# Second third's token tiles ahead of its weights, and the last two LRU blocks beside the attention's later heads

## The chip, the cores and the metric

The kernel runs on one core of a Trainium2 chip. The time is device microseconds of one execution. The engines are TensorE (PE; its weight loads are PEld), VectorE (DVE), ScalarE (ACT), GpSimd (POOL) and SyncE (SP, which issues nearly all DMAs).

## The reference, cut to what matters

One layer of a hybrid trunk, 2048 tokens of width 1024 with 16 meta tokens ahead of them, in float32. An input projection feeds three groups of heads; their outputs go together into an output projection, and a feed-forward layer follows.

```python
h += rms_norm(w_out @ concat(rg_lru_group, forgetting_attention_group, rwkv7_group), g_post)   # all read w_in @ rms_norm(h)
h += rms_norm(w_down @ (gelu(g) * v))            # [g | v] = causal_dwconv3(w_up @ rms_norm(h))

def rg_lru_group(xa, ya, ...):                   # the gated linear recurrence, 256 wide
    u = causal_dwconv(xa, conv_w) + conv_b       # 4 taps
    r = sigmoid(u @ ga_w + ga_b); i = sigmoid(u @ gx_w + gx_b)
    log_a = -8.0 * r * softplus(-lam)
    a = exp(log_a); b = sqrt(-expm1(2 * log_a)) * (i * u)
    h = scan(h_t = a_t * h_{t-1} + b_t)
    return h * gelu(ya)

def forgetting_attention_group(...):             # 8 heads of 64
    s = qh @ kh.T + (c_q - c_k)                  # c: running sum of log_sigmoid(f)
    return softmax(causal(s)) @ vh

def rwkv7_group(...):                            # 4 heads of 64, a state of 64 x 64 a head
    S = S * w_t - (S @ kk_t) (kk_t * a_t)^T + v_t k_t^T;  o_t = S @ r_t
```

## The kernel before

The work goes through five stages: input projection, attention, output projection, and the two halves of the feed-forward layer.

The input projection runs in three thirds of the tokens ("parts" 0 to 2; tiles of 128 tokens 0 to 7, 7 to 13, 13 to 17). For each third, `w_in_norm` loads token tiles (`token_load`), normalises them and transposes them on TensorE (L161). Then `w_in_part` takes the weight columns one after the other. In part 0 it splits each weight tile into a high and a low part and keeps both in memory (`scr_wk`); parts 1 and 2 load them back (L259, tiles `wh` and `wl`). The loads, and most stores, are issued by SP in the order in which they stand.

Beside the projection's matmuls run the recurrences. The tokens are cut in nine blocks, 0 to 8; the last is a short one of one chunk, 64 tokens. `recurrences` makes three blocks a third: the RWKV block (`R.block`, whose tail `R.ending` is run one block later) and the LRU block (`lru_block`). What is left over when the projection is written is written ahead of the attention, and `rec`, the group of memory pools that the recurrences use, is closed there.

An LRU block runs twice, for channels 0 to 127 and 128 to 255 (`p` 0 and 1). Each of the two passes loads its input (`rwlraw`, L1549), applies the convolution on ScalarE (L1556) and with three VectorE operations (L1558), two gate matmuls on TensorE (L1563, L1564), then some twenty operations on ScalarE and VectorE, among them a square root with a table of its own on ScalarE (L1579, the exponential's is loaded again after it), a scan on VectorE (L1581), the product with the second input (L1585 to L1590) and a store (L1591). The gates' result lies in a PSUM bank of the recurrences, `eps`.

The tail of an RWKV block, as far as it is spoken of here: solves with small matmuls (L1316), L1360 to L1412, the outputs (L1443, L1448), a normalisation on VectorE with an inverse square root of small steps (L76 to L84, L1453 to L1461), a transpose and a gate (L1468, L1472), L1475, L1479, L1480 and the store of the result (L1482).

The attention has two halves. Half 0 takes blocks 0 and 1 of 512 queries for all eight heads, half 1 blocks 2 and 3. For each head and block, `maxima` computes the row maxima of the scores (matmul L644 into a bank `mx`, VectorE L649, transpose L659, ScalarE L660), and `weights` computes the scores again (L773, L774, bank `sc`), their exponentials (ScalarE L778, tile `p`) and the product with the values (L796, bank `po`). From head 5 of half 0 on (`WIDE`), there are three `mx` banks instead of two. At each piece `Attn.tick` is called; every second tick takes a step of a generator `beside`, which in half 1 is the meta tokens' part.

The order on each engine is made ahead of the run by a scheduler: it takes the instructions in the order in which the code writes them, knows which waits for which and when memory comes free, and lets later work go ahead of work that waits. `issue_after(x)` keeps an instruction behind instruction `x`. Pools marked `early` may lie on memory whose former user is still at work; the first write then waits.

Of the kernel before, what the change touches and what calls it, by code (L numbers as in the profile page):

```python
# [1 line left out]

# [6 lines left out]
F32 = mybir.dt.float32  # L9
# [9 lines left out]
P = 128  # L19
# [13 lines left out]
class Core:  # L33


    def __init__(self, tc, ctx):
        self.tc = tc
        self.nc = tc.nc
        self.ctx = ctx
        self.uid = 0  # L40
        nc = self.nc
        self.const = ctx.enter_context(tc.tile_pool(name="const", bufs=1))
        self.ident = self.const.tile([P, P], F32, name="ident")
        make_identity(nc, self.ident[:])
        self.flip = 0
        self.root = self.apart = False
        self.power, self.held = None, []
        self.turns = 0
# [84 lines left out]
def token_load(core, pools, src, rows):  # L133

    xt = pools["nt"].tile([P, D], F32, tag="nt_x", name=core.n("xt"))
    core.nc.sync.dma_start(xt[:rows], src)
    return xt


# [96 lines left out]
def w_in_kept(scr, c0):  # L236

    return scr["wk"][c0 // P]


def w_in_weights(core, pools, w_in, c0, scr, part, raw=None, behind=False):

    src = w_in[:, c0 : c0 + P].rearrange("(k p) c -> p k c", p=P)
    if raw is not None:
        pair = hi, lo = [pools["w"].tile([P, KD, P], F32R, tag=s, name=core.n(s)) for s in ("wh", "wl")]
        core.loaded = core.nc.sync.dma_start(raw, src)
        with core.tc.issue_after(core.high.ins) if behind else nullcontext():
            core.rounded = core.nc.scalar.activation(hi[:], raw, AF.Copy)
        with core.tc.issue_after(core.low.ins) if behind else nullcontext():
            core.nc.vector.tensor_tensor(lo[:], raw, hi[:], op=ALU.subtract)  # L250
    elif part == 0:
        pair = split_load(core, pools["w"], (pools["nt"], "nt_x", None), src, [P, KD, P], "w")
    else:
        core.turns += part == 2
        pl, tags = (pools["nt"], ("nt_x", "nt_x")) if core.turns % 4 > 1 else (pools["w"], ("wh", "wl"))
        pair = [pl.tile([P, KD, P], F32R, tag=tag, name=core.n(s)) for s, tag in zip(("wh", "wl"), tags)]
    for t, kept in zip(pair, w_in_kept(scr, c0)):
        t = t[:].rearrange("p k c -> p (k c)").bitcast(F32)
        core.loaded = core.nc.sync.dma_start(*((kept, t) if part == 0 else (t, kept)))  # L259
    return pair  # L260


# [248 lines left out]
class Attn:  # L511
# [63 lines left out]
    def t(self, shape, tag, dt=F32, bufs=2):  # L575
        return self.pool.tile(shape, dt, tag=tag, name=self.core.n(tag), bufs=bufs)
# [335 lines left out]
    def run(self, pool, third):  # L912


        self.queue = self.nc.sync
        ready = []
        for half, bs in enumerate(((0, 1), (2, 3))):
            if half:
                self.rear(third, "k2_2")
                self.beside = self.meta(pool)  # L920
            for h in range(NH):
                self.wide = (half, h) >= WIDE
                with self.core.tc.issue_after(self.core.settled) if not half and h < 2 else nullcontext():
                    keys = self.keys(h, 4 * bs[-1] + 5)
                for b in bs:
                    gen, total, out = self.maxima(h, b, keys), self.pieces(b), []

                    def fill(share, gen=gen, total=total, out=out):
                        while len(out) < min(total, share * total):
                            out.append(next(gen))  # L930

                    if len(ready) == self.AHEAD:
                        self.weights(*ready.pop(0), fill)
                    fill(1.0)
                    ready.append((h, b, keys, next(gen)))
                    self.serial += 1
                    self.later.append((self.clock + self.FINISH, self.serial, lambda gen=gen: next(gen, None)))
                    self.later.sort(key=lambda x: x[:2])
                    if len(ready) < self.AHEAD + 1 and not half and h == 0:
                        next(gen)  # L940
        self.tail = True
        for i, step in enumerate(ready):
            if i == len(ready) - 1:
                self.queue = self.nc.gpsimd
            self.weights(*step, lambda share: None)
        self.flush()
        for _ in self.beside:
            pass
        while len(self.later) > 1:
            self.later.pop(0)[2]()  # L950
# [644 lines left out]

class Banks:


# [554 lines left out]
PACE = 1.25  # L2155

WIDE = (0, 5)

LATE, NORMS = 8, 2

# [35 lines left out]
def recurrences(core, R, lk, f_bias, scr, blocks, part):  # L2196


    for blk in blocks:
        gate_block(core, R, f_bias, scr, blk[2])  # L2200
        yield
    for b in ((0, 1, 2), (3, 4, 5), (6, 7, 8))[part]:
        gen = R.block(b)
        while next(gen) != R.SOLVED:
            yield
        yield from R.ending
        R.ending = gen
        yield from lru_block(core, R, scr, lk, b)


_INS = [
# [9 lines left out]
def hybrid_block_kernel(ctx: ExitStack, tc: tile.TileContext, args, out):  # L2221
    a = {s: v[0] if s != "meta_tokens" else v for s, v in args.items()}
    nc = tc.nc
    core = Core(tc, ctx)
    scr = scratch(tc, ctx, core)
# [8 lines left out]
    def pool(es, name, bufs, **kw):  # L2234
        return es.enter_context(tc.tile_pool(name=name, bufs=bufs, **kw))

    right = {"side": "right"}
    early = {"reuse_waits": "tile"}
# [8 lines left out]
    with ExitStack() as p1:  # L2247
# [2 lines left out]
        rec = ExitStack()  # L2250
        ps_rw = pool(rec, "ps_rw", 2, space=PSUM, **right)
        ps_ae = pool(rec, "ps_ae", 1, space=PSUM, **right)
        rc = pool(rec, "rc", 1, **right)
        gp = pool(rec, "gp", 1, **right)
        rp = pool(rec, "rp", 1, **right)
        with ExitStack() as p1a:
# [14 lines left out]
            for part in range(3):  # L2271
# [7 lines left out]
                if part == 0:  # L2279
# [5 lines left out]
                    with tc.issue_after(core.powered.ins):  # L2285
# [9 lines left out]
                            for s, v in a.items() if s.startswith("rwkv_")  # L2295
                        },
                    )
                    lk = lru_consts(
                        core, gp, ps_ae,
                        {  # L2300
# [8 lines left out]
                    R = Rwkv(core, rp, dp, ps_rw, ps_ae, scr, rk)  # L2309
# [30 lines left out]
        with ExitStack() as p1b:  # L2340
            more = pool(p1b, "ps_more", 1, space=PSUM, **right, **early)
            front = pool(p1b, "front", 2, **early)
            ps_at = pool(p1b, "ps_at", 1, space=PSUM, **early)
            ap = pool(p1b, "ap", 2, **early)
            with tc.issue_after(core.parted):
                at = Attn(core, ap, ps_at, more, scr, front)
            at.second = pool(p1b, "ap2", 1, **early)

            pool(p1b, "pad", 1, **right).tile([P, 23872], F32, name="pad")
            at.run(pool(p1b, "mt", 1, **right, **early), pool(p1b, "k2", 1, **right, **early))  # L2350
    qp = pool(ctx, "qp", 1, **early)
    gf = pool(ctx, "gf", 1, **early)
    with ExitStack() as p3:
# [12 lines left out]
        with p2:  # L2366
# [9 lines left out]
            for i, (f, rows) in enumerate(FFN_TILES):  # L2376
# [12 lines left out]
                for _ in range(NORMS if i > LATE else 0):  # L2389
                    if todo:  # L2390
                        q, f, rows = todo.pop(0)
                        xt = ffn_fetch(core, np_, scr, f, rows)
# [144 lines left out]
```

## Time and profile before

| What | Value |
|---|---|
| Runs, us | 2953.79, 2942.76, 2957.45 (median 2953.79) |
| Profiled execution, us | 2948.27, span 2946.6, mean granted clock 0.98 |
| Busy share of the span | PE 96%, PEld 83%, DVE 68%, ACT 51%, POOL 44% |
| Share of the chain that ended last | PE 69%, DVE 8%, DMA 5%, ACT 5% |
| First to second third of the projection | 258 to 292 us |
| Attention, half 0 | from 849 us, half 1 written from about 1068 us |

The times count from the span's start. A row of the timeline has start, length, engine, line, operation, and in brackets how long the engine was idle before it and what ended that. PEclk is the share of full speed that TensorE's clock was granted.

### The profile page before, as it was taken

The page shows a single profiled execution, that of the slowest core. Times are in us where ns is not written, and L with a number is a line of the kernel's source. Part 1 is how long each engine was busy: PE and PEld are TensorE (multiplying, and loading weights), DVE is VectorE, ACT ScalarE, POOL GpSimd, SP SyncE. Part 2 cuts the span into 40 slices and gives each one's busy share as a digit, 9 for nine tenths or more (in the row PEclk, how much of TensorE's full clock was granted, in tenths as well). Part 3 has the DMA queues.
Part 4 walks back from the last instruction along what each step waited for, and adds up shares of the span by engine and source line. Part 5 has one row for each costly group of instructions (what it writes and reads, how often), then busy time and mean ns, then how long its engine had stood idle before and what let it go on. Part 6 is the DMA issues. An engine that isn't in the chain of part 4 may idle for free.

```text
span 2946.6 us, 53222 instructions
## 1 busy us (share of the span) xinstructions
PE 2832.0 (96%) x18854; PEld 2441.3 (83%) x18854; DVE 1997.5 (68%) x3839; ACT 1504.0 (51%) x2937; POOL 1302.6 (44%) x1572
## 2 busy tenths in 40 slices
PE   8999999989988889999999999999999999999998
PEld 8998989978965555666578999999999999787887
DVE  4357654665678665556656988888787787656766
ACT  3246442554446554555645666666666665324333
POOL 1002221222114567667624666456655444656443
PEclk9999999999989899999999999999999999999999
DMA  7775678577643357445264665577767764436453
GB/s 244 250 243 190 220 232 289 181 234 244 204 122 79 79 130 222 100 121 128 49 192 148 210 195 179 157 231 210 220 200 223 215 198 148 141 112 218 151 171 122
DMA packets 470344, 530.51 MB, mean 180 GB/s; under 512 B 86863, under 2 KB 356889, under 8 KB 468525
## 3 DMA queue, kind: packets, MB, share of 16 engines
q1 hardware_dynamic: 469308, 526.18, 59.1%
q8 instruction: 148, 2.42, 0.4%
q0 software_dynamic: 768, 0.93, 0.1%
q14 instruction: 120, 0.98, 0.1%
HBM read 368.07 MB, written 158.90 MB: 179 GB/s over the span
## 4 chain that ended last, share of the span: by engine, by line
PE 69%; DVE 8%; DMA 5%; ACT 5%; issue 2%; POOL 2%; SPq 1%; DVEq 0%; POOLq 0%; ACTq 0%
PE psu L193 10%; PE psu L194 9%; PE psu L195 9%; PE psd L193 4%; PE psd L194 4%; PE psd L195 4%; PE po L796 4%; PE psp L193 2%; PE psp L195 2%; PE psp L194 2%; PE mx L644 2%; PE sc L773 2%; PE pswo L193 2%; PE pswo L194 2%; PE pswo L195 2%
## 5 line engine op out<-in xcount | busy, mean ns | idle before, releaser
L194 PE MATMUL psu<-xo,uw 128*128 128x344 f32 x1848 | 592.0, 321 | 0.0
L193 PE MATMUL psu<-xo,uw 128*128 128x344 f32 x1848 | 586.6, 322 | 3.3 <-DVE vb L1971 2.2
L195 PE MATMUL psu<-xo,uw 128*128 128x344 f32 x1848 | 582.4, 320 | 0.6 <-DVE uw L1780 0.6
L193 PE MATMUL psp<-xh,wh 128*128 128x384 f32 (+2 forms) x1152 | 379.9, 330 | 0.7 <-DMA wh<-scr_wk 0.7
L194 PE MATMUL psp<-xl,wh 128*128 128x384 f32 (+2 forms) x1152 | 374.8, 325 | 0.0
L195 PE MATMUL psp<-xh,wl 128*128 128x384 f32 (+2 forms) x1152 | 373.2, 324 | 0.0
L1780 DVE TENSOR_TENSOR uw<-uq,uw 128x512 fp32r<-128x512 f32 x341 | 313.6, 924 | 61.6 <-ACT uw L1779 58.1
L193 PEld LDWEIGHTS psu<-xo,uw 128*128 128x128 f32 x1848 | 346.1, 188 | 4.7 <-DVE vb L1971 2.7
L194 PEld LDWEIGHTS psu<-xo,uw 128*128 128x128 f32 x1848 | 347.4, 188 | 0.0
L195 PEld LDWEIGHTS psu<-xo,uw 128*128 128x128 f32 x1848 | 346.0, 188 | 1.4 <-DVE uw L1780 1.4
L1779 ACT ACTIVATE uw<-uq 128x512 fp32r<-128x512 f32 x462 | 287.8, 627 | 104.8 <-PE psu L195 46.0
L778 ACT ACTIVATE p<-sc,bias 128x512 f32<-128x512 f32 (+4 forms) x352 | 197.3, 590 | 161.6 <-PE sc L774 138.0
L649 DVE TENSOR_REDUCE mc<-mx 128x1 f32<-128x512 f32 (+5 forms) x352 | 191.6, 566 | 113.8 <-PE mx L644 81.0
L1919 DVE SCALAR_TENSOR_TENSOR uy<-psu,ffn_cols,uy 128x342 f32<-128x342 f32 (+1 forms) x390 | 220.8, 567 | 64.6 <-ACT uy L1917 62.2
L1927 POOL TENSOR_TENSOR uy<-uy,uy 128x342 f32<-128x342 f32 (+1 forms) x132 | 146.9, 1113 | 229.5 <-DVE uy L1919 69.3
L1780 POOL TENSOR_TENSOR uw<-uq,uw 128x512 fp32r<-128x512 f32 x121 | 184.8, 1527 | 132.6 <-ACT uw L1779 113.2
L193 PEld LDWEIGHTS psp<-xh,wh 128*128 128x128 f32 x1152 | 218.2, 189 | 6.5 <-issue 3.4
L194 PEld LDWEIGHTS psp<-xl,wh 128*128 128x128 f32 x1152 | 218.4, 190 | 5.5 <-issue 4.0
L195 PEld LDWEIGHTS psp<-xh,wl 128*128 128x128 f32 x1152 | 218.2, 189 | 4.4 <-issue 3.1
L817 POOL TENSOR_TENSOR acc<-acc,p 128x512 f32<-128x512 f32 (+3 forms) x186 | 197.0, 1062 | 47.4 <-DVE acc L817 22.6
L1780 DVE TENSOR_TENSOR fo<-u,fo 128x896 fp32r<-128x896 f32 x88 | 101.2, 1150 | 131.7 <-ACT fo L1779 131.2
L1779 ACT ACTIVATE fo<-u 128x896 fp32r<-128x896 f32 x88 | 81.2, 923 | 209.2 <-PE psd L195 112.9
(492 smaller groups left out, 6288.3 us busy)
## 6 DMA issues: line engine op xcount, KB each, us to landing
uq<-scr_us SPq DMA_DIRECT2D x220, 256.0 KB
uq<-in_ffn_up_dram SPq DMA_DIRECT2D x209, 256.0 KB
wl<-scr_wk SPq DMA_DIRECT2D x48, 512.0 KB
wh<-scr_wk SPq DMA_DIRECT2D x48, 512.0 KB
u<-scr_ff SPq DMA_DIRECT2D x88, 256.0 KB
scr_ff<-uy SPq DMA_DIRECT2D x110, 171.0 KB
raw<-in_w_in_dram SPq DMA_DIRECT2D x24, 512.0 KB
scr_wk<-wh SPq DMA_DIRECT2D x24, 512.0 KB
```

The lines of the kernel that those rows point to most:

```text
L193: nc.tensor.matmul(out, ah, bh, start=first, stop=False, skip_group_check=more)
L194: nc.tensor.matmul(out, ah, bl, start=False, stop=False, skip_group_check=more)
L195: nc.tensor.matmul(out, al, bh, start=False, stop=last, skip_group_check=more)
L644: nc.tensor.matmul(ps[:rows, : e - a], q3[:, qo : qo + rows], k2[:, a:e], start=True, stop=not last)
L649: self.reduced = nc.vector.tensor_reduce(mc[:rows, i, ci : ci + 1], ps[:rows, : e - a], axis=AX.X, op=ALU.max)
L778: last = nc.scalar.activation(p[:rows, :w], ps[:rows, :w], AF.Exp, bias=bias[:rows, j : j + 1])
L796: mm = nc.tensor.matmul(po[at : at + 64, c0:n], v1[:rows, j], p[:rows, : n - c0], start=start and i < 2, stop=end and i + 2 >= len(group), ...
L817: eng.tensor_tensor(a, ps_[0][0][:rows, c0:n] if start and i == 1 else a, p[:rows, : n - c0], op=ALU.add)
L1779: core.nc.scalar.activation(hi, src, AF.Copy)
L1780: (eng or core.nc.vector).tensor_tensor(lo, src, hi, op=ALU.subtract)
L1919: core.conved = stt(y[:, :n], src[:, i : n + i], cw[:, 44 * i + cc : 44 * i + cc + 1], y[:, :n], op0=ALU.mult, op1=ALU.add)
L1927: core.pooled = nc.gpsimd.tensor_tensor(v[:, :n], g[:, :n], v[:, :n], op=ALU.mult)
```

## The change

Two things change. First, in part 1 the loads of the kept weights (L259) are held behind the DMA of the last token tile that was loaded (`core.token`), which is the second third's last tile.

Second, LRU blocks 7 and 8 leave `recurrences`. They become a generator `at.rest`, which the attention's ticks step from head 5 of half 0 on (`RESUME`), and which is run to its end before half 1. Its tiles come from a pool of its own, `lr`, which is early, and the gates use a bank of the `mx` ring instead of `eps`. The LRU's constants move to a pool `lc` that outlives the recurrences, and the pool `k2` is opened only after `lr` is closed.

```diff
-    core.nc.sync.dma_start(xt[:rows], src)
+    core.token = core.nc.sync.dma_start(xt[:rows], src)
...
-        core.loaded = core.nc.sync.dma_start(*((kept, t) if part == 0 else (t, kept)))
+        with core.tc.issue_after(core.token.ins) if part == 1 else nullcontext():
+            core.loaded = core.nc.sync.dma_start(*((kept, t) if part == 0 else (t, kept)))
...
             if half:
-                self.rear(third, "k2_2")
+                for _ in self.rest:
+                    pass
+                self.rear(third(), "k2_2")
                 self.beside = self.meta(pool)
             for h in range(NH):
+                if (half, h) == RESUME:
+                    self.beside = self.rest
...
+class Spare:
+
+    def __init__(self, core, pool, at):
+        self.core, self.pool, self.pe = core, pool, at.mx
+
+    def t(self, shape, tag, bufs=1):
+        return self.pool.tile(shape, F32, tag=tag, name=self.core.n("rw" + tag), bufs=3 if tag == "lu" else bufs)
...
+LAST, RESUME = (7, 8), (0, 5)
...
-        yield from lru_block(core, R, scr, lk, b)
+        if b not in LAST:
+            yield from lru_block(core, R, scr, lk, b)
...
+        lc = pool(p1, "lc", 1, **right)
...
+                    core.const = lc
                     lk = lru_consts(
...
-            pool(p1b, "pad", 1, **right).tile([P, 23872], F32, name="pad")
-            at.run(pool(p1b, "mt", 1, **right, **early), pool(p1b, "k2", 1, **right, **early))
+            pool(p1b, "pad", 1, **right).tile([P, 23872 - 536], F32, name="pad")
+            mt = pool(p1b, "mt", 1, **right, **early)
+            early_half = p1b.enter_context(ExitStack())
+            spare = Spare(core, pool(early_half, "lr", 1, **right, **early), at)
+            at.rest = chain(*(lru_block(core, spare, scr, lk, b) for b in LAST))
+
+            def third():
+                early_half.close()
+                return pool(p1b, "k2", 1, **right, **early)
+
+            at.run(mt, third)
```

What it does to the order is seen at three places. In the changed kernel the line numbers are higher by 2 near L640 and L800 and by 6 from L1300 to L1600; L1564 there is L1558 before, and L1569 and L1570 are the gates' L1563 and L1564.

TensorE, where the maxima of head 5 of half 0 are taken, before. The last two outputs of RWKV block 7 (L1468, L1472) and the first step of block 8's tail (L1316):

```order
L1468 MATMUL rps_10969<-ident,rww_1248_9855 128x128 x2
L1472 MATMUL rps_10972<-rwsg_9696,g_up 128x256
L644 MATMUL mx_12350<-k_1402_11222,q_1405_11235 128x128
L646 LDWEIGHTS identb
L646 MATMUL mx_12350<-futureb,identb 128x128
L1468 MATMUL rps_10977<-ident,rww_1248_9855 128x128 x2
L644 MATMUL mx_12399<-k_1402_11222,q_1403_11227 128x400
L659 MATMUL mx_12331<-ident,sh_12329 1x128 x4
L1472 MATMUL rps_10980<-rwsg_9696,g_up 128x256
L644 MATMUL mx_12406<-k_1402_11222,q_1403_11227 128x400
L774 MATMUL sc_12382<-q_1407_11241,k_1402_11222 128x512
L774 MATMUL sc_12387<-q_1407_11241,k_1402_11222 128x512
```

The same place now, with the beginning and then the end of the stretch:

```order
L775 MATMUL sc_12276<-q_1638_11998,k_1381_11096 128x512
L1474 MATMUL rps_10896<-ident,rww_1248_9858 128x128 x2
L1478 MATMUL rps_10899<-rwsg_9699,g_up 128x256
L1474 MATMUL rps_10904<-ident,rww_1248_9858 128x128 x2
L1478 MATMUL rps_10907<-rwsg_9699,g_up 128x256
L1322 MATMUL rps_10926<-rwxu_10913,rwsc_10521 32x32 x8
L1322 MATMUL rps_10936<-rwxu_10913 32x32 x4
```

```order
L1474 MATMUL rps_11045<-ident,rwxu_11006 128x64
L1478 MATMUL rps_11047<-rwsg_10433,g_up 128x64
L1569 MATMUL mx_12152<-rwlu_12144,lru_ga_w 128x256
L1570 MATMUL mx_12152<-rwlu_12144,lru_gx_w 128x256
L646 MATMUL mx_12185<-k_1374_11073,q_1377_11086 128x272
```

Between the two pieces stand 12 more rows, all of RWKV block 8. The attention's pieces that stood between the tail's steps now stand behind the first gates of LRU block 7.

SP, at the same place, before and now. Before, block 8's store (L1482) has loads for the attention around it:

```order
L634 DMA q_1407_11241<-scr_ql 64x512
L1482 DMA scr_mix<-rwxu_11155 128x2x64
L612 DMA v_1410_11246<-scr_v 128x16x64
L861 DMA scr_rden<-dcol_12704 16x32
L867 DMA scr_mix<-o_12615 64x512
```

```order
L615 DMA v_1385_11104<-scr_v 16x64
L1488 DMA scr_mix<-rwxu_11006 128x2x64
L1555 DMA rwlraw_12142<-scr_p 128x259
L1555 DMA rwlraw_12234<-scr_p 128x256
L688 DMA mt_13039<-scr_kh 64x8x16
```

The inputs of LRU block 7's first pass (`rwlraw`) are now loaded directly behind that store, and loads of the meta tokens' part (`mt`) follow.

SP, between the first and the second third of the projection, before and now (`fw`: weights of the forget gates, `us`: rows of the feed-forward weights, `xt`: token tiles, `sth` and `stl`: results of the first third):

```order
L329 DMA fw_3228<-scr_wk 128x1024
L259 DMA wl_3402<-scr_wk 128x1024
L281 DMA scr_qh<-sth_3017 128x384
L282 DMA scr_ql<-stl_3018 128x384
L1804 DMA us_3556<-in_ffn_up_dram 128x2x128 x4
L259 DMA wh_3401<-scr_wk 128x1024
L259 DMA wl_3567<-scr_wk 128x1024
L281 DMA scr_qh<-sth_3068 128x384
L282 DMA scr_ql<-stl_3069 128x384
L136 DMA xt_3184<-in_x_dram 128x1024
L136 DMA xt_3206<-in_x_dram 128x1024
```

```order
L331 DMA fw_3231<-scr_wk 128x1024
L283 DMA scr_qh<-sth_3020 128x384
L284 DMA scr_ql<-stl_3021 128x384
L283 DMA scr_qh<-sth_3071 128x384
L137 DMA xt_3187<-in_x_dram 128x1024
L284 DMA scr_ql<-stl_3072 128x384
L137 DMA xt_3209<-in_x_dram 128x1024
L261 DMA wh_3404<-scr_wk 128x1024
L261 DMA wl_3405<-scr_wk 128x1024
L1634 DMA raw_3557<-in_w_out_dram 128x1024
L1819 DMA us_3559<-in_ffn_up_dram 128x2x128 x4
```

The two token tiles stand ahead of the weights and of the four `us` loads now.

More of the change, by code (lines that the diff above doesn't have):

```diff
@@ L1 @@
 from contextlib import ExitStack, nullcontext
+from itertools import chain
 import concourse.bass as bass
```

## The prediction

> **What bounds the kernel now.** I read the busy times and the chain that ended last first, then the granted clock and the busy time by stretches around the two places of the change, then the idle time of TensorE there, row by row. The page says where time is worth something:
>
> ```profile
> PE 2832.0 (96%) x18854; PEld 2441.3 (83%) x18854; DVE 1997.5 (68%) x3839; ACT 1504.0 (51%) x2937; POOL 1302.6 (44%) x1572
> PE 69%; DVE 8%; DMA 5%; ACT 5%; issue 2%; POOL 2%; SPq 1%; DVEq 0%; POOLq 0%; ACTq 0%
> ```
>
> TensorE is the bound: its 114.6 us of idle time in 2946.6, and its time at half clock, are all that an order can win. The stretches around place B (first half of the attention; columns: start and end, length, busy us with counts of PE, PEld, DVE, ACT, POOL, then granted clock, DMA share, GB/s):
>
> ```profile
> 850.00:985.00 135.00, 110.31 (x1200) 75.92 (x1195) 109.90 (x304) 81.38 (x184) 56.89 (x100) 0.83 0.43 103
> 985.00:1018.90 33.90, 28.62 (x288) 19.38 (x284) 23.49 (x67) 15.68 (x33) 23.43 (x38) 0.95 0.28 69
> 1018.90:1075.00 56.10, 52.06 (x349) 32.83 (x349) 38.80 (x118) 34.12 (x70) 34.97 (x52) 0.92 0.59 130
> ```
>
> In the first stretch, where blocks 7 and 8 of the LRU run now, TensorE idles 24.7 us at a mean clock of 0.83, and VectorE is as busy as TensorE. In the third it hardly waits.
>
> **Place A, the token tiles.** TensorE's longest wait between the first two thirds of the projection:
>
> ```profile
> 265.75 1.31 SPq L136 DMA_DIRECT2D xt<-in_x_dram  x2
> 272.35 1.06 ACT L124 ACTIVATE xj<-xt 128x1024 bf16<-128x1024 f32 x1 [4.22 <-DMA xt<-in_x_dram]
> 269.51 1.02 DVE L1199 SCALAR_TENSOR_TENSOR rwbk<-rwe 128x512 f32<-128x512 f32 x1
> 270.58 0.79 PE L1231 MATMUL rps<-rwrav,rwbk 64*128 64x128 f32 x2 [6.54 <-DVE rwbk L1199]
> 277.81 3.11 PE L161 MATMUL pst<-ident,xt 128*128 128x128 f32 x16
> 270.50:277.80 7.30, 7.21 (x26) 3.87 (x27) 4.80 (x9) 3.21 (x6) 2.70 (x3) 0.50 0.68 254
> ```
>
> The two tiles are issued late (265.75) and ScalarE waits 4.22 us for them, but TensorE does not: its 6.54 us end with VectorE's L1199, an operation of the RWKV group, and from there to the tiles' transposes (L161) it is busy 7.21 of 7.30 us, at half clock. The changed order of TensorE still has those RWKV matmuls ahead of the last 16 transposes. So the earlier tiles are worth nothing by themselves. What moves is VectorE: the tile's 0.15 us L127 now stands ahead of L1199, and one of three L168 of the row that ends at 269.51 stands behind it. That brings L1199 forward by at most 0.6 us, or, if the tile lands late, holds it up. The four `us` loads and the weight loads that are passed on SP's queue have room: the weights are needed at 292. I take -0.5 us, between -1 and +2.
>
> **Place B, what leaves the early heads.** TensorE's waits that end with something of LRU blocks 7 and 8, or with a VectorE or ScalarE operation queued directly behind it, and the clock after two of them:
>
> ```profile
> 895.99 0.45 PE L773 MATMUL sc<-q,k 128*128 128x400 f32 x1 [1.87 <-ACT p L778]
> 912.13 0.70 PE L644 MATMUL mx<-k,q 128*128 128x400 f32 x1 [2.93 <-DVE lru_h L1582]
> 963.02 0.39 PE L773 MATMUL sc<-q,k 128*128 128x272 f32 x1 [1.72 <-ACT p L778]
> 974.14 0.24 PE L1316 MATMUL rps<-rwxf,rwxu 32*32 32x32 f32 x2 [1.25 <-DVE rwxu L1346]
> 981.64 0.59 PE L644 MATMUL mx<-k,q 128*128 128x272 f32 x1 [3.31 <-DVE mc L649]
> 978.52 2.60 DVE L1589 SCALAR_TENSOR_TENSOR rwlr<-rwlr,rwlraw 128x64 f32<-128x64 f32 x1 [1.66 <-ACT rwlr L1588]
> 891.60 1.28 ACT L1579 ACT_TABLE_LOAD   x1
> 912.10:916.00 3.90, 2.81 (x13) 1.75 (x15) 3.34 (x9) 3.44 (x9) 2.50 (x3) 0.50 0.01 2
> 916.00:920.00 4.00, 4.00 (x41) 3.54 (x39) 2.93 (x10) 2.04 (x6) 0.83 (x2) 0.68 0.20 59
> 981.60:986.00 4.40, 4.36 (x28) 3.48 (x30) 1.69 (x5) 0.00 (x0) 1.42 (x4) 0.50 0.05 11
> ```
>
> The five waits sum to 11.1 us. After the two long ones the clock is down: 2.81 x 0.5 + 4.00 x 0.32 + 4.36 x 0.5 = 4.9 us of matmul time lost. Together 16.0. Part of it stays, since the RWKV operations of blocks 7 and 8 and the attention's own sums stand in the same queues and are late next; I take 13. The ends: 5 (the clock and half of the waits stay), and 25 (every idle us of the stretch goes).
>
> [...] The trace shows 0.50 after a wait of 2.93 us. [...]
>
> **Place B, what becomes exposed.** In the changed order the two sets of LRU gates stand on TensorE behind the whole tail of RWKV block 8, and nothing of the attention stands inside that tail. Their input is loaded by SP, in order, behind the store of block 8's output (L1482). Before, the tail has attention pieces between all its steps. Its rows, with a load's latency and the first LRU steps from where they stand now:
>
> ```profile
> 1016.58 2.25 DVE L1461 TENSOR_TENSOR rww<-rww,rwgsm 128x512 f32<-128x512 f32 x1
> 1018.89 0.69 PE L1468 MATMUL rps<-ident,rww 128*128 128x128 f32 x2 [3.66 <-DVE rww L1461]
> 1023.17 0.42 DVE L1480 TENSOR_TENSOR rww<-rww,rps 128x256 f32<-128x256 f32 x1
> 1024.52 0.33 PE L1316 MATMUL rps<-rwxu,rwsc 32*32 32x32 f32 x16
> 1050.42 0.15 DVE L78 SCALAR_TENSOR_TENSOR rwgsm<-rwgsm 64x4 f32<-64x4 f32 x1
> 1050.61 0.16 DVE L79 TENSOR_TENSOR rwgsm<-rwgsm 64x4 f32<-64x4 f32 x1
> 1062.20 0.43 PE L1472 MATMUL rps<-rwsg,g_up 128*128 128x64 f32 x2
> 1062.67 0.22 DVE L1480 TENSOR_TENSOR rwxu<-rwxu,rps 128x64 f32<-128x64 f32 x1 [0.45 <-PE rps L1472]
> 1063.62 0.53 SPq L1482 DMA_DIRECT2D scr_mix<-rwxu  x1
> 810.35 0.33 SPq L1549 DMA_DIRECT2D rwlraw<-scr_p  x1
> 813.08 0.59 ACT L1556 ACTIVATE rwlu<-rwlraw,lru_cols 128x256 f32<-128x256 f32 x1
> 813.90 0.48 DVE L1558 SCALAR_TENSOR_TENSOR rwlu<-rwlraw,lru_cols,rwlu 128x256 f32<-128x256 f32 x1
> ```
>
> - Block 7's last outputs: L1468 at 1018.89 to the second L1480, 4.7 us with attention between. Alone about 3.8.
> - Block 8: L1316 at 1024.52 to the last L1480's end at 1062.89, 38.4 us, most of it waiting behind attention. Alone, by the rows' own durations: 31 VectorE operations of 10.8 us in all, 9 where the few of 1.0 to 1.2 take what their lines take otherwise, 9 on ScalarE of 3, 12 steps of TensorE on the chain of 5, and some 20 handovers of 0.1. That is 19 us, an estimate from the rows from L1316 to L1480, of which the first and last are shown.
> - From L1480 to the gates: 0.73 to L1482's issue, 0.55 of it, 2.73 from a load's issue to ScalarE's L1556 (810.35 to 813.08), 0.59, and three L1558 (1.4): 6.0.
>
> The chain is 3.8 + 19 + 6 = 29 us (24 if every handover is as short as 0.04, as between the two 0.15 us rows; 33 if the half clock stretches TensorE's steps and SP is late). TensorE's own work in it is 21 rows of 10.7 us, from L1468 at 1018.89 to L1472 at 1062.20; the rest is idle time that the attention no longer fills.
>
> **Place B, what comes to the later heads.** All of LRU 7 and 8 now stands between the chain's end and the end of half 0. What that brings, from 875 to 985 (the ScalarE rows from 810 to 990, which also count a pass of block 6):
>
> ```profile
> L1579 ACT ACT_TABLE_LOAD x5 | 6.4, 1283 | 0.1
> L778 ACT ACT_TABLE_LOAD x3 | 3.8, 1283 | 0.1
> L1573 ACT ACTIVATE rwla<-rwlr,lru_rate 128x256 f32<-128x256 f32 (+1 forms) x5 | 2.2, 442 | 4.7 <-DVE rwlr L1570 4.7
> L1588 ACT ACTIVATE rwlr<-rwlr 128x256 f32<-128x256 f32 (+1 forms) x5 | 1.7, 349 | 1.6 <-DVE rwlr L1587 1.5
> L1589 DVE SCALAR_TENSOR_TENSOR rwlr<-rwlr,rwlraw 128x256 f32<-128x256 f32 (+1 forms) x4 | 4.8, 1194 | 2.2 <-ACT rwlr L1588 2.2
> ```
>
> ScalarE: 8 table loads, 10.2 us (the changed order has eight too), and nine operations and an L1556 a pass, of 0.35 to 0.5 us in the mean, four passes, 15.4: 25.6, of which 1.1 runs before the first gates. VectorE: 14 groups, of which the costliest is shown, 27 us.
>
> The stretch 1018.90 to 1075.00 without block 8's tail and with the LRU in it: TensorE 52.1 - 10.7 = 41.4 of work, 4.0 of the waits that stand there now and 2.5 for a clock that restarts low after the chain, 48. ScalarE 34.1 - 3.9 (the tail's rows there) + 24.5 = 55. VectorE 38.8 - 12 (the tail's) + 26 = 53. ScalarE sets it, with the exps behind its table loads; I take 56, just above its own work, because TensorE's score banks keep no more than two pieces ahead of it. The ends are 48 (all of it beside) and 62 (ScalarE 90% busy). SP's moved loads and stores (8 and 4) are issued between mt and q loads that are needed later; nothing on POOL moves here.
>
> **Sum.** Now 56.1 us from 1018.90 to 1075.00; then 29 + 56 = 85, which is +28.9. Less 13 in the early heads, less 0.5 at place A: +15.4. The profiled execution took 2948.27 us (span 2946.6), so 2963.7 against it. It lies 5.5 under the median of the runs, 2953.79, from which I count: 2969. That is about the 0.5% (14.8 us) that a measurement of this kernel can tell from no change.
>
> **Rivals.**
> - *Not slower: the relief is the larger* (chance 0.20). For: VectorE is 81% busy from 850 to 985, and 27 us of its work leave. If all 24.7 us of idle time go and the later heads take the LRU beside their work (48), it is 29 + 48 - 56.1 - 25 - 0.5 = -4.6: 2949. It decides from a relief above 21 us. Against: only 11.1 us of the waits lie directly behind LRU operations.
> - *The later heads choke* (0.22): LRU operations hold the mx banks and the table loads stand between exps. 33 + 62 - 56.1 - 10 - 0.5 = +28: 2982. For: ScalarE 55 against TensorE's 41. Against: order places only eight gates' matmuls there.
> - *Short chain* (0.10): 24 + 50 - 56.1 - 13 - 0.5 = +4: 2958. For: VectorE and POOL have nothing beside the chain, and operations that stand at 1.0 to 2.3 us now may take 0.15 to 0.7.
> - The token tiles' part failing (VectorE waiting at L127) moves none of these by more than 2.
>
> **Chances and range.** The forecast has 0.48, and covers +8 to +22: 2962 to 2976. Half of it and a little is above the bound. Slower: 0.22 + 0.26 = 0.48; faster: two fifths of the first rival, 0.08; the rest, 0.44, is within 0.5%. The range leaves out the better half of the first rival and the worst of the second: 2948 to 2988.
>
> **What would show it.** In the changed trace: a stretch near 1000 us where TensorE is less than half busy for 25 to 30 us, with waits that end with block 8's VectorE operations and one of 5 to 6 us that ends with L1558 (line 1564 there), then clock 0.5. No wait on L1582 or L1589 before it, and TensorE idle 10 to 14 us less from 850 to there. ScalarE near 90% busy behind the first gates. L1199's wait 6 us still at place A. I am wrong if the chain's idle time is under 12 us, or if the early heads give back 20.

## The result, and the profile after

| What | Before | After |
|---|---|---|
| Median, us | 2948.88 (five runs, 2942.76 to 2957.45) | 2988.65 (six runs, 2983.99 to 2993.92) |
| Ratio, 95% interval | | 1.013 [1.0114, 1.0146] |
| Profiled execution, us | 2948.27, span 2946.6 | 2987.06, span 2985.3 |

The change makes the kernel 39.8 us slower by these medians, 34 to 43 by the interval. A sixth run of the kernel before took 4872.87 us and is left out. The forecast had the direction (+15.2), but less than half of the size; 2988.65 lies 0.65 above the end of its range.

The page of the changed kernel, its busy times and the shares of the chain that ended last:

```profile
PE 2848.9 (95%) x18854; PEld 2445.4 (82%) x18854; DVE 2002.7 (67%) x3839; ACT 1505.5 (50%) x2937; POOL 1303.1 (44%) x1572
PE 66%; DMA 8%; DVE 7%; ACT 5%; POOL 3%; issue 3%; SPq 1%; DVEq 0%; POOLq 0%; ACTq 0%
```

The instructions are as many as before (18854 matmuls, 3839 on VectorE). TensorE is busy 16.9 us longer for the same matmuls, at a mean granted clock of 0.975 where it was 0.980, and idle 21.8 longer (136.4 of 2985.3 where it was 114.6 of 2946.6). In the chain DMA rises from 5% to 8% and PE falls from 69% to 66%. Three per cent of the span are 90 us, more than twice the loss, so these shares do not say where it lies.

At place A hardly anything moved. TensorE's wait there, after:

```profile
270.07 0.79 PE L1237 MATMUL rps<-rwrav,rwbk 64*128 64x128 f32 x2 [5.66 <-DVE rwbk L1205]
```

It was 6.54, ending at 270.58; it ends 0.51 sooner. The loss is in half 0 of the attention. Its stretches by engine (columns as in the prediction's windows: length, busy us of PE, PEld, DVE, ACT, POOL, granted clock, DMA share, GB/s), after:

```profile
850.00:1012.60 162.60, 133.81 (x1441) 91.21 (x1440) 111.03 (x318) 75.86 (x172) 80.17 (x138) 0.86 0.42 100
1012.60:1039.30 26.70, 13.25 (x126) 9.26 (x126) 12.15 (x45) 4.47 (x12) 2.29 (x4) 0.55 0.27 58
1039.30:1107.00 67.70, 53.86 (x215) 31.99 (x216) 45.68 (x119) 48.85 (x100) 33.59 (x48) 0.75 0.36 82
```

and the same two parts before, split where the tail's first row (L1468) begins:

```profile
850.00:1018.90 168.90, 138.93 (x1484) 95.30 (x1477) 133.39 (x371) 97.06 (x217) 80.33 (x138) 0.85 0.40 96
1018.90:1068.70 49.80, 45.95 (x327) 29.40 (x327) 34.91 (x106) 30.66 (x65) 32.41 (x49) 0.94 0.55 127
```

The last window of each ends where VectorE's first cast of half 1's keys starts, in the timeline of after and of before:

```profile
1107.05 1.11 DVE L568 CAST k<-ident 64x520 fp32r<-64x520 f32 x3
1068.70 1.69 DVE L566 CAST k<-ident 64x520 fp32r<-64x520 f32 x3
```

Behind these ends little differs: 1878.3 us with 9908 matmuls are left after, 1877.9 with 9903 before. At the end of the first window, too, the two kernels are equally far: 74 of the 352 row-maximum matmuls (`mx<-k,q`) are done in both.

So the account is: the early stretch is 6.3 us shorter (162.6 against 168.9), the tail of RWKV block 8 stands alone for 26.7, and from the first gates to half 1 it takes 67.7 where 49.8 did before, with the tail inside them. The sum is -6.3 + 26.7 + 17.9 = +38.3, of 38.7 between the two spans.

The rows of the middle, in the changed kernel's timeline (start, length, engine, line, operation, and in brackets the idle time before it and what ended it):

```profile
1012.59 0.41 PE L1474 MATMUL rps<-ident,rww 128*128 128x128 f32 x2 [0.86 <-DVE rww L1467]
1032.02 0.34 PE L1474 MATMUL rps<-ident,rwxu 64*128 64x64 f32 x1 [4.46 <-DVE rwxu L1467]
1034.41 0.36 SPq L1488 DMA_DIRECT2D scr_mix<-rwxu  x1
1034.82 0.46 SPq L1555 DMA_DIRECT2D rwlraw<-scr_p  x1
1037.10 0.60 ACT L1562 ACTIVATE rwlu<-rwlraw,lru_cols 128x256 f32<-128x256 f32 x1 [3.38 <-DMA rwlraw<-scr_p]
1039.31 1.22 PE L1569 MATMUL mx<-rwlu,lru_ga_w 128*128 128x256 f32 x2 [5.19 <-DVE rwlu L1564]
```

The first load of LRU block 7 (L1555) is issued 0.05 us after the issue of block 8's store (L1488) ends, and the gates come 4.5 us behind that. Between 1012.59 and 1039.31 no row of the attention stands on TensorE. Its idle time in those 26.7 us is 13.45.

### The profile page after: what moved, and what is told of

Same layout as the page of the kernel before. It is cut to its first block, busy times and chain, and to the rows that moved or that the text cites. A ratio compares the mean times of both kernels' runs of the same rounds, so it can differ in the third digit from the quotient of the medians.

```text
span 2985.3 us, 53225 instructions
## 1 busy us (share of the span) xinstructions
PE 2848.9 (95%) x18854; PEld 2445.4 (82%) x18854; DVE 2002.7 (67%) x3839; ACT 1505.5 (50%) x2937; POOL 1303.1 (44%) x1572
## 4 chain that ended last, share of the span: by engine, by line
PE 66%; DMA 8%; DVE 7%; ACT 5%; POOL 3%; issue 3%; SPq 1%; DVEq 0%; POOLq 0%; ACTq 0%
PE psu L194 9%; PE psu L195 9%; PE psu L196 9%; PE psd L194 4%; PE psd L195 4%; PE psd L196 4%; PE po L798 3%; PE psp L194 3%; PE psp L195 3%; PE psp L196 3%; PE pswo L194 2%; PE pswo L196 2%; PE pswo L195 2%; PE sc L775 1%; PE mx L646 1%
## 5 line engine op out<-in xcount | busy, mean ns | idle before, releaser
L780 ACT ACTIVATE p<-sc,bias 128x512 f32<-128x512 f32 (+4 forms) x352 | 197.6, 591 | 174.3 <-PE sc L776 146.7
L651 DVE TENSOR_REDUCE mc<-mx 128x1 f32<-128x512 f32 (+6 forms) x352 | 191.3, 566 | 104.3 <-PE mx L646 71.0
```

The costliest lines, as they stand in the source:

```text
L651: self.reduced = nc.vector.tensor_reduce(mc[:rows, i, ci : ci + 1], ps[:rows, : e - a], axis=AX.X, op=ALU.max)
L780: last = nc.scalar.activation(p[:rows, :w], ps[:rows, :w], AF.Exp, bias=bias[:rows, j : j + 1])
```

## Experiments

All of them are made from the changed kernel, but for the token tiles' part alone, which is made from the kernel before. Differences are between medians, to the kernel before as it ran beside each, unless another is named.

### One part alone

The token tiles' part alone, on the kernel before:

```diff
+    core.token = core.nc.sync.dma_start(xt[:rows], src)
...
+        with core.tc.issue_after(core.token.ins) if part == 1 else nullcontext():
```

> The first part of the change alone: the token tiles ahead of the second third's weights, the LRU as before. Theory M (the loss is all in the attention): no change, 2951 us, within 3. Rival S (the weights that now come later hold the second third up, and the attention only passes that on): 2960 or more.

Measured: 2942.42 against 2953.53, ratio 0.9965 [0.9946, 0.9984], and once more

> The first part alone once more, with more rounds, as the version that ran fastest: 0.9945 to 0.9985 of the kernel before if its gain is real, 1.000 if it was chance.

2940.62 against 2950.68, ratio 0.9975 [0.9958, 0.9992]. This part alone makes the kernel 10 to 11 us faster, twice (7 to 10 by the ratios), and it is the version that beats both kernels. The first expectation was a miss. The wait at place A cannot have brought it: there, 0.5 us moved. The first 150 us of the attention, before, with this part alone, and in the second profile of the same version:

```profile
850.00:1000.00 150.00, 123.73 (x1343) 85.80 (x1336) 117.63 (x330) 87.91 (x197) 65.20 (x114) 0.84 0.42 101
850.00:1000.00 150.00, 128.36 (x1381) 86.12 (x1383) 122.73 (x349) 95.32 (x215) 79.69 (x136) 0.92 0.46 111
850.00:1000.00 150.00, 128.92 (x1319) 87.08 (x1317) 116.29 (x331) 94.33 (x212) 71.86 (x123) 0.85 0.45 107
```

In the first of the two profiles (an execution of 2937.46 us) TensorE does more there (128.36 us at 0.92 instead of 123.73 at 0.84: 118 us at full clock instead of 104, an estimate as busy time times clock), though the edit touches only loads of the projection. TensorE's order in the attention's first half came out otherwise. In the second profile (2946.13 us) the same order ran at 0.85, 110 us at full clock, so part of the 14 us is the execution that was profiled and not the edit. I read the gain as a by-product of the order; that it arises here is not shown, and which of the moved rows brings it was not separated.

The other part alone, the changed kernel without the token edit:

```diff
-        with core.tc.issue_after(core.token.ins) if part == 1 else nullcontext():
-            core.loaded = core.nc.sync.dma_start(*((kept, t) if part == 0 else (t, kept)))
+        core.loaded = core.nc.sync.dma_start(*((kept, t) if part == 0 else (t, kept)))
```

> The second part of the change alone: LRU blocks 7 and 8 moved, the token tiles' loads as before. Theory M: the loss is this part's, 2983 to 2999. Since the first part alone ran 10 us faster than the kernel before, adding the parts up would give 2998; if the first part's gain was a by-product of the order that the scheduler found for the attention, it need not add up, and 2988 is as likely. Rival S (both parts are needed for the loss): 2965 or less.

Measured: 2986.56 against 2950.68, ratio 1.012 [1.0092, 1.0149]. The loss is this part's. The tail begins and the gates wait as in the whole change (line numbers one lower):

```profile
1010.16 0.41 PE L1473 MATMUL rps<-ident,rww 128*128 128x128 f32 x2 [1.07 <-DVE rww L1466]
1037.00 1.22 PE L1568 MATMUL mx<-rwlu,lru_ga_w 128*128 128x256 f32 x2 [5.17 <-DVE rwlu L1563]
```

The parts do not add up (-10 and +36 would be +26, and it is +40): where the LRU is moved as well, the token part's gain is not to be found.

### How much is the LRU, and how much the wait

The LRU of blocks 7 and 8 only loaded and stored (`lru_bare`: the load, a yield, the store), and then the same with the two gate matmuls between:

```diff
-            at.rest = chain(*(lru_block(core, spare, scr, lk, b) for b in LAST))
+            at.rest = chain(*(lru_bare(core, spare, scr, b) for b in LAST))
```

> The changed kernel with the computation of LRU blocks 7 and 8 left out: their rows are loaded and stored again, with no gates, no scan and no ScalarE or VectorE work (so this part of the output is not computed). The order interleaves the tail of RWKV block 8 with the attention again. It shows what the early heads gain. Theory M: 13 to 20 us under before, 2931 to 2938. Rival R (LRU work was hidden before; its place matters little): within 5 of before.

Measured: 2940.46 against 2953.53, ratio 0.9958 [0.9941, 0.9975]. I had expected 2931 to 2938, and the rival a time within 5 us of before; neither came. With no LRU work at all in the attention the kernel is 13 us under the kernel before, but only 2 us under the one that has the token tiles' part and keeps the LRU among the early heads (2942.42, run beside it). This version has the token edit as well, and the two parts do not add up. So these runs put the LRU's leaving the early heads at 2 to 13 us and do not settle it; the traces give 6 to 9 (below).

> As the one before, but each of the four passes still loads its input, runs its two gate matmuls into a bank of the mx ring and takes them out with one ScalarE operation; the rest of LRU 7 and 8 is left out. TensorE's order has the whole tail of RWKV block 8 in one piece ahead of the first gates, as in the changed kernel. Theory M: the exposed tail by itself costs 20 to 25 us against the kernel without LRU 7 and 8, so about 2957. Rival R (the loss is the LRU's ScalarE and VectorE work, with its table loads, beside heads 5 to 7; the tail's idle time is given back): within 6 of the kernel without LRU 7 and 8.

Measured: 2963.03, ratio 1.0028 [1.0016, 1.0039]. The two gate matmuls of each of the four passes, with a bank of the `mx` ring and one ScalarE operation, cost 22.6 us over the kernel without them. Its timeline shows the same chain:

```profile
1010.21 0.41 PE L1474 MATMUL rps<-ident,rww 128*128 128x128 f32 x2 [0.87 <-DVE rww L1467]
1029.71 0.34 PE L1474 MATMUL rps<-ident,rwxu 64*128 64x64 f32 x1 [4.45 <-DVE rwxu L1467]
1034.87 1.22 PE L1551 MATMUL mx<-rwlu,lru_ga_w 128*128 128x256 f32 x2 [3.06 <-DMA rwlu<-scr_p]
```

From L1474 to the gates 24.7 us, of which 22.6 show in the time. That is the price of the exposed tail. The rest of the loss comes with the LRU's own operations behind the gates: 25.6 us between the two medians (2988.65 and 2963.03), 30.3 between the two differences to the kernel before (+39.8 and +9.5).

### Which wait: the bank, the memory or the pool

The gates in a bank of the output projection's pool instead of the `mx` ring:

```diff
-            spare = Spare(core, pool(early_half, "lr", 1, **right, **early), at)
+            spare = Spare(core, pool(early_half, "lr", 1, **right, **early), ps_wo[0])
...
+        return self.bank.tile([P, 512], F32, tag="wo", name=self.core.n("gates"), bufs=2)
```

> The changed kernel whole, but the LRU's gates lie in a PSUM bank of their own (one that the output projection uses later) instead of the mx ring. All work is done. The order has the tail of RWKV block 8 between attention pieces again, and the LRU behind it, squeezed into head 7. Theory M: the tail's 22 us are back; what stays is the LRU's work beside the last head, 10 to 17: about 2945 to 2955. Rival R: 2980 or more, since the LRU's work now stands even closer together.

Measured: 2976.64 against 2953.53, ratio 1.0075 [1.0052, 1.0098], neither what the one nor what the other theory expected. SP's issues and TensorE's waits in its timeline:

```profile
1052.68 0.54 SPq L1488 DMA_DIRECT2D scr_mix<-rwxu  x1
1055.72 0.82 SPq L1555 DMA_DIRECT2D rwlraw<-scr_p  x2
1082.72 0.69 PE L1569 MATMUL gates<-rwlu,lru_ga_w 128*128 128x64 f32 x2 [10.57 <-DVE rwlu L1564]
1091.82 0.66 PE L1569 MATMUL gates<-rwlu,lru_ga_w 128*128 128x64 f32 x2 [7.98 <-DVE rwlr L1583]
1109.61 0.67 PE L646 MATMUL mx<-k,q 128*128 128x400 f32 x1 [16.71 <-DMA k<-scr_cl]
```

Out of the ring the gates no longer hold up the attention, which now stands inside the tail (the tail's last L1474 waits 1.80 us instead of 4.46). But the LRU's first load still stands behind block 8's store on SP, which now comes 18.3 us later (1052.68 against 1034.41). Then the LRU runs with little beside it, and half 1, whose `k2` lies on the memory of `lr`, waits for it: 35 us of idle time in three waits. As I read it, the bank decides only where the wait is paid; what makes it is the late load.

The LRU's tiles of all blocks in a pool `lp` that is open from the projection through the attention, the gates in the `mx` ring as in the change, from head 5 as in the change:

```diff
+        lp = pool(p1, "lp", 1, **right)
...
+                    R.lru = Spare(core, lp, R.pe)
...
-            early_half = p1b.enter_context(ExitStack())
-            spare = Spare(core, pool(early_half, "lr", 1, **right, **early), at)
+            k2 = pool(p1b, "k2", 1, **right, **early)
+            spare = Spare(core, lp, at.mx)
```

> The changed kernel whole, with one thing different: the LRU's tiles, for all nine blocks, come from a pool of their own that stays open from the projection through the attention, instead of from the recurrences' pools first and from the early pool lr, opened behind them, for blocks 7 and 8. Same work, same ring for the gates, same start at head 5. In its order the tail of RWKV block 8 stands between attention pieces, and the four gate pairs stand beside it. Theory M (the loss is the chain that comes of waiting for the recurrences' memory: the exposed tail, and then the LRU squeezed between it and half 1): both go, 2938 to 2948. Rival R (LRU work beside heads 5 to 7 costs its 25 us wherever the tail stands): 2963 or more.

Measured: 2950.85 against 2954.29, ratio 0.9999 [0.9985, 1.0014]. The loss of 1.3% is gone, although the LRU runs in the same heads, with the same ring and the same square roots. The time is 3 us above theory M's range and 12 under the rival's. A load of the LRU's input, the gates and the tail in its timeline:

```profile
996.43 0.54 SPq L1555 DMA_DIRECT2D rwlraw<-scr_p  x1
1008.64 0.70 PE L1569 MATMUL mx<-rwlu,lru_ga_w 128*128 128x256 f32 x2
1015.23 0.64 PE L1474 MATMUL rps<-ident,rww 128*128 128x128 f32 x2
1028.68 0.43 PE L1569 MATMUL mx<-rwlu,lru_ga_w 128*128 128x64 f32 x2 [0.40 <-DVE rwlu L1564]
1050.05 0.33 PE L1569 MATMUL mx<-rwlu,lru_ga_w 128*128 128x64 f32 x2
```

The load is issued 38 us earlier than in the changed kernel (1034.82), ahead of the tail and of its store. The first gates stand ahead of the tail's L1474 at 1015.23, the last come at 1050.05, and the longest wait before one of these rows is 0.40 us. It does not reach the token part alone (-10 to -11, where this is -3.4, or 0 by the ratio): as far as one order of each tells, the LRU is no cheaper in the later heads than where it stood.

To see whether the bytes or the pool are waited for, `lr` was put on addresses whose last user is the LRU of block 6, long done, but still opened where the change opens it:

```diff
-            pool(p1b, "pad", 1, **right).tile([P, 23872 - 536], F32, name="pad")
+            pool(p1b, "pad", 1, **right).tile([P, 5448], F32, name="pad")
+            spare = Spare(core, pool(p1b, "lr", 1, **right, **early), at)
+            pool(p1b, "pad2", 1, **right).tile([P, 16088], F32, name="pad2")
...
+            k2 = pool(p1b, "k2", 1, **right, **early)
```

> The changed kernel with the pool lr at other addresses: those that the recurrences' own LRU tiles had, whose last user is LRU block 6, long before. It is still opened behind the closed pools of the recurrences; k2 no longer waits for lr. The order has the tail of RWKV block 8 in one piece ahead of the gates again, and the load of LRU block 7's input behind block 8's store on SP. Theory M1 (it is the closed pools as a whole that are waited for, not the bytes): as the changed kernel, 2980 to 2992. Theory M2 (the wait is on the bytes that lr and k2 lie on): 2945 to 2960.

Measured: 2979.5 against 2950.68, ratio 1.0104 [1.0078, 1.013]. 28.8 of the 39.8 us stay, 2979.5 is 0.5 under theory M1's range and 19.5 above M2's, and the waits are the changed kernel's:

```profile
1025.68 0.34 PE L1474 MATMUL rps<-ident,rwxu 64*128 64x64 f32 x1 [4.46 <-DVE rwxu L1467]
1032.99 1.22 PE L1569 MATMUL mx<-rwlu,lru_ga_w 128*128 128x256 f32 x2 [5.20 <-DVE rwlu L1564]
```

So it is not the former user of these bytes that `lr` waits for, if the addresses are as I counted them; no view shows them. Both this version and the one with its own pool open `k2` ahead and take one buffer for the tile `lu` where the change takes three; since this one keeps most of the loss, neither of these is what the own pool wins by. That `k2` no longer waits for `lr` may be what is gone here, 8 us by the ratios and 11 by the medians; that was not tried. As far as these two runs tell, a pool that is opened behind the closed recurrence pools gets its first tile after the last work in them, block 8's tail, wherever it lies.

### The table loads

The square root of blocks 7 and 8 replaced by a tanh, which stands among the exponentials with no table load (L1594 at 1055.54 and L780 at 1055.86 in the changed kernel's timeline):

```diff
-        nc.scalar.activation(r, r, AF.Sqrt)
+        nc.scalar.activation(r, r, AF.Tanh if b in (7, 8) else AF.Sqrt)
```

> The changed kernel with the square root of LRU blocks 7 and 8 replaced by a tanh, which is in the table that the exps use, so that the eight table loads of 1.28 us go (this part of the output is not the reference's). Theory M (the LRU's steps behind the tail are a chain of handovers; the loads are 10 us of it, partly beside other work): 4 to 10 under the changed kernel, 2979 to 2985. Rival R2 (the table loads between the exps are what the later heads lose): 15 or more under it, 2974 or less.

Measured: 2979.49 against 2954.29, ratio 1.01 [1.0075, 1.0126], 9 us under the changed kernel by the two medians, 15 by the differences to the kernel before. The two intervals overlap, so the size is uncertain; it fits theory M, and none of the four runs (2976.21 to 2988.45) comes down to the rival's 2974. So the loads are a third to a half of what the LRU's operations cost, by these two counts. One of them on ScalarE in the changed kernel's timeline:

```profile
1047.02 1.27 ACT L780 ACTIVATE p<-sc,bias 128x512 f32<-128x512 f32 x2 [0.57 <-PE sc L776]
1048.30 1.28 ACT L1585 ACT_TABLE_LOAD   x1
1049.59 0.42 ACT L1585 ACTIVATE rwlr<-rwlr 128x256 f32<-128x256 f32 x1
```

The load takes 1.28, and what stands before and after it follows within 0.01. From 1000 to 1130 us the changed kernel has eight loads, of 1283 ns in the mean: 10.3 us. The version with the tanh has none there.

### Other places, with the own pool

From head 2 on (`RESUME = (0, 2)`), and in half 1 behind the meta tokens' part (`self.beside = chain(self.meta(pool), self.rest)`):

> As the one before, with the LRU's steps from head 2 on instead of head 5. Theory M: the place hardly matters once nothing waits, within 6 of the one before. Rival R: it stands in the early heads again, where the unchanged kernel has it, so as that one, 2951.

Measured: 2972.02 against 2954.29, ratio 1.0072 [1.0048, 1.0095], a miss.

> As the two before, with the LRU's steps in the attention's second half, behind the meta tokens' part. Theory M: as the kernel without LRU 7 and 8, 2938 to 2946. Rival R: 2963 or more, since its table loads stand between as many exps.

Measured: 2967.52 against 2954.29, ratio 1.0051 [1.0032, 1.007], a miss too. The first stretch of the attention, with the own pool from head 5 and from head 2:

```profile
850.00:1000.00 150.00, 135.74 (x1409) 92.25 (x1409) 102.71 (x296) 75.43 (x171) 82.39 (x140) 0.85 0.43 101
850.00:1000.00 150.00, 125.18 (x1322) 85.53 (x1324) 113.90 (x330) 85.58 (x193) 63.38 (x111) 0.81 0.41 100
```

From head 2, TensorE is busy 10.6 us less up to 1000 us, at a lower clock. But that is not where the loss stays: of the 352 row-maximum matmuls (L646, tile `mx<-k,q`), the first starts 8 us later than with the own pool from head 5 (852.0 against 843.6), the 111th, near the end of half 0, 2 us (1078.7 against 1076.9), and the last 24 us (1470.2 against 1445.9). Most of it comes behind half 0, where neither of the two has LRU work. With the LRU in half 1, the 301st of them starts 8 us behind that of the kernel without LRU work (1381.5 against 1373.9), and the last 27 (1465.4 against 1438.5). Why these places cost 13 to 18 us is not settled.

## Why the prediction was right and wrong

- **Place A, -0.5:** right. The wait stayed (5.66), and the row behind it starts 0.51 earlier. That the same edit alone makes the kernel 10 us faster, which the wait at place A cannot explain, was in no case of mine.
- **Exposed chain, 29 (24 to 33):** right in kind and size: 26.7, with TensorE busy 13.25. I had counted 10.7 us of TensorE's own work in it and 6.0 from L1480 to the gates. The experiment with the gates alone puts 22.6 us on it. The half clock (0.55) and the wait of 5.19 ending with L1564 are there as named. But I read the wait from the order only; why the load stands behind the tail, the pool, I had not asked.
- **Relief in the early heads, -13 (5 to 25):** the first step that failed, by its size. The stretch is 6.3 us shorter, 8.7 with the LRU's part alone (1010.16 against 1018.89 for the tail's first row), and its idle time fell by 1.2 (28.8 of 162.6, from 30.0 of 168.9), not by 10 to 14; the clock is 0.86 instead of 0.85. I summed the waits that ended with LRU operations or with something queued behind them, and their clock. The waits on L1582 and L1589 are gone as I said, but others took their place. Of the three longest in the changed kernel's timeline, one ends with a load of the attention's queries and two with RWKV's and the attention's own operations on VectorE:

```profile
855.50 1.10 PE L775 MATMUL sc<-q,k 128*128 128x512 f32 x2 [3.59 <-DMA q<-scr_qh]
978.60 2.00 PE L1410 MATMUL rps<-rww,rwsc 128*64 128x64 f32 x32 [3.22 <-DVE rwrav L1400]
995.35 1.13 PE L646 MATMUL mx<-k,q 128*128 128x400 f32 x2 [4.12 <-DVE mc L651]
```

  Keeping 13 of 16 was the error: I named what is late next and gave it 3. Of the 4.9 us for the clock, 2.2 were misread besides. The half clock that I put behind the wait of 3.31 us (978.33 to 981.64) had begun ahead of that wait, in the kernel before:

```profile
976.60:981.60 5.00, 1.62 (x8) 1.23 (x6) 3.30 (x7) 3.79 (x9) 3.87 (x7) 0.50 0.09 30
```

- **Later heads, 56 (48 to 62):** the step that cost most, and the one whose mechanism was wrong: I let ScalarE's work set the time. The forecast's 56 went to 1075.00; up to half 1's cast, at 1068.70 before, it is 49.7. Measured: 67.7, so 18 too low. TensorE is idle 13.8 us of it (3.9 in the 49.8 before) and busy 53.86 (45.95 before): 10 from waits and 8 from matmuls at 0.75 of full clock instead of 0.94, although the tail's matmuls are no longer in it. ScalarE is busy 48.85 of 67.70, 72%, not near 90%: it is not throughput but handovers. TensorE's two largest groups of waits from 1039.3 to 1113 (total us, times, longest), and the longest single wait with the two ScalarE rows ahead of it:

```profile
PE sc L775 <- ACT p L780: 5.5, 6, 2.5
PE mx L646 <- DVE mc L651: 5.2, 6, 1.5
1085.03 1.28 ACT L780 ACT_TABLE_LOAD   x1
1086.32 0.69 ACT L780 ACTIVATE p<-sc,bias 128x512 f32<-128x512 f32 x1
1087.06 0.57 PE L775 MATMUL sc<-q,k 128*128 128x272 f32 x1 [2.46 <-ACT p L780]
```

  Scores wait for exponentials that stand behind LRU operations and table loads on ScalarE; the one at 1086.32 has the LRU's L1585 and L1591 (1082.88 and 1083.42) ahead of it, and a table load (1.28 at 1085.03), of which the version without the square root has none. Maxima wait for reductions that stand behind LRU operations on VectorE: L1586, L1587 and L1592 run between 1069.65 and 1071.89, ahead of the reduction that ends the wait of 1.46 us at 1072.42. With the own pool the same operations are spread from before 1008 us, and the kernel takes as long as the kernel before.
- **The sum:** -0.5 - 13 + 29 + (49.7 - 49.8) = +15.4 was forecast; by the same terms it came to -6.3 + 26.7 + 17.9 = +38.3. Of the miss of 23, 7 is the relief, 18 the later heads, and -2 the chain.
- **The rivals:** nearest was "the later heads choke", +28. Its mechanism was right in part: LRU operations and table loads stand between the exps. Held banks were not it: only one wait, of 0.54 us at 1043.64, ends with an LRU operation that frees a bank of the `mx` ring (L1573), and with the gates in another bank the kernel still lost. Its price for the later heads (62) was still too low. "Not slower" fell with its relief of 25, and "short chain" with 26.7 against 24.

## What to carry to other kernels

When work is moved to a later place in its own new pool, ask first what that pool's first write waits for: here the pool stood behind the last work in pools that had been closed, so four moved passes made a hidden tail visible; with the pool opened ahead of them, the same move lost nothing that could be measured (ratio 0.9999). Price a stretch that mixes two chains by its handovers and the clock after them, not by the busiest engine's sum (here ScalarE was 72% busy, and the clock 0.75), and price a relief by what is late next: an engine's wait for an operation is not won in full by removing that operation (here 1.2 us of idle time went where 10 to 14 were forecast). An edit can bring 10 us that the waits at its own place do not explain, as the token loads did here, so time the parts alone before giving any of them the credit.

## What the runs showed of the hardware

In one place of the changed kernel the clock stood at 0.50 for 8 us behind two waits of 1.4 and 1.0 us. Windows of 4 us:

```profile
1094.00:1098.00 4.00, 1.62 (x10) 0.99 (x8) 2.62 (x11) 3.94 (x7) 1.97 (x3) 0.92 1.10 247
1098.00:1102.00 4.00, 3.98 (x14) 1.98 (x15) 0.99 (x4) 1.56 (x6) 1.58 (x6) 0.50 0.80 157
1102.00:1106.00 4.00, 4.00 (x16) 3.05 (x15) 3.27 (x10) 2.60 (x6) 3.96 (x4) 0.50 0.24 74
1106.00:1110.00 4.00, 4.00 (x18) 2.10 (x17) 2.64 (x7) 1.86 (x4) 0.62 (x2) 0.80 0.87 190
```

TensorE's waits in these 16 us, grouped (total us, times, longest), are two, in or at the end of the first window:

```profile
PE mx L646 <- ACT acc L856: 1.4, 1, 1.4
PE sc L775 <- ACT p L780: 1.0, 1, 1.0
```

TensorE is busy 1.62 of those 4.00 us. Then the clock is 0.50 for 8 us in which it is busy 3.98 and 4.00 of 4.00. The matmul time lost, an estimate from these rows, is 3.98 x 0.5 + 4.00 x 0.5 + 4.00 x 0.2 = 4.8 us, twice the 2.4 of the waits. The later heads ran at 0.75 with no wait above 2.5 us behind the first gates; this is the one place of theirs that was taken apart. The half clock does not always last that long. Earlier in the same trace it lasted at most 3.5 us by these windows, and TensorE was busy for all of the 3.30 in the middle one:

```profile
930.00:933.50 3.50, 1.09 (x7) 0.83 (x7) 3.33 (x11) 1.10 (x3) 2.73 (x5) 1.00 0.24 62
933.60:936.90 3.30, 3.30 (x14) 2.09 (x14) 2.33 (x9) 0.39 (x2) 2.31 (x4) 0.50 0.16 38
937.00:940.40 3.40, 2.89 (x19) 1.86 (x16) 1.66 (x2) 3.14 (x7) 2.67 (x4) 1.00 0.37 118
```

Ahead of the one TensorE was busy 1.62 of 4.00 us, ahead of the other 1.09 of 3.50. What makes the difference between them was not tried.
